# When finished activation tiles are written out to DRAM: four chunks after their first product in place of 28

## The chip, the cores and the metric

The kernel runs on one core of a Trainium2 chip. The metric is the time on the device in microseconds (us), the median of several runs. A run's time is a little longer than its span, the stretch that the profiler records.

## The reference, cut to what matters

One layer of a streaming encoder on 512 tokens of width 1024. A mixer (convolutions and a gated recurrence) comes first; behind it stands a retrieval over 128 × 128 = 16384 small "experts". Each token needs 8 × 16 of them:

```python
idx = ...                      # (tokens, 8 heads, 16): experts chosen by a two-stage top-16
g = softmax(best_s)            # their gates
u_sel = expert_u[idx]
act = gelu(einsum('phkd,pd->phk', u_sel, xb))
coef = g * act
return einsum('phk,phkd->pd', coef, expert_v[idx])
```

`expert_u` and `expert_v` are tables of 16384 × 1024 numbers, 64 MB each.

## The kernel before, in words

The 512 tokens are split. For 192 of them the chosen rows of the tables are gathered one by one (indirect DMAs issued by POOL, tile `rows`) and multiplied on DVE (`scr` at L918 for the u table, `ys` at L935 for the v table). For the other 320 the kernel computes densely: it takes the u table in 128 chunks of 128 experts, forms all products of a chunk with the 320 tokens on TensorE (PE), applies the gelu, multiplies by a gate that is zero for experts that were not chosen, and multiplies by the chunk of the v table.

The work follows a list `jobs`: chunks 0 to 123 of u come first ("u phase"); then the 128 chunks of v ("v phase"), with the last four chunks of u between the first of them. Around job k the program is written out by hand, and each engine keeps that order:

- `w_ahead` lets the SP queue issue the 512 KB loads of table chunks, five or six jobs ahead, into a ring of four buffers `wraw` (L70; in the v phase every fifth goes to a buffer `raw`, L962, and chunks 5 to 11 of u go straight into `whi` or `wlo` buffers, L957).
- `w_high(k + 3)` lets ACT round the chunk to its high half `whi` (L75); `w_low(k + 2)` lets DVE form the low half `wlo` (L80). Both rings have four buffers, so a half of chunk k can be written once PE is done with chunk k − 4, and a `wraw` buffer is free once DVE has made the low half.
- `u_chunk(k)` issues 24 matmuls into `ps_act` (L89 to L91, or L1011 in chunks 1 to 11), and then `u_evict` puts the gelu of the chunk before into SBUF (ACT, L1002). Two chunks share one tile `act`, a pair: 128 × 640 numbers, 320 KB. There are 16 such tiles.
- The v phase begins with pair 48. Pairs 0 to 47 are written to DRAM (`spill`, L992, tensor `Ad`, issued by SP) and read again later in the v phase (`v_act`, L1064). Pairs 48 to 63 stay in SBUF.

Beside this, DVE and ACT search the top-16 lists and build the gate tables, which go out to DRAM through SP (`Gd<-stg`, L786). At the end of the u phase SP fetches the first gates (`gt<-Gd`, L1051, six loads of 512 KB) and later ones in loads of 1 MB (`h<-Gd`, L1038). In the v phase `v_gated` forms the coefficients `cf` (ACT L1072, DVE L1074), `v_high` and `v_rest` split them into `ch` (ACT, L1081) and `cl` (DVE, L1088), and PE adds up `acc` (L1197), 18 matmuls for a chunk. In both phases DVE's program has steps of the gathers (`scr`, `ys`) between the others.

SP is one queue: it issues its DMAs in program order, and one that has to wait holds up those behind it. All DMAs share the 16 DMA engines.

In `u_chunk(c)` for an even chunk c, `spill(q)` is called with q = c // 2 − RB // 2 + 2; RB is 32, so pair q goes out in chunk 2q + 28. The condition `0 <= q < v0 // 2` with v0 = 96 limits it to pairs 0 to 47.

Of the kernel before, what the change touches and what calls it, by code (L numbers as in the profile page):

```python
# [34 lines left out]
def block_kernel(ctx, tc, xT, small, w_ada1, w_ada, b_ada, w_in, w_r, w_i, w_out, w_q, keys, uT, u, v, final_g, out):  # L35
# [51 lines left out]
    def mm3(ps, hi, lo, xh, xl, ks, first, last):  # L87
        for k in ks:
            nc.tensor.matmul(ps, hi[:, k, :], xh(k), start=first and k == ks[0], stop=False)  # L89
            nc.tensor.matmul(ps, hi[:, k, :], xl(k), start=False, stop=False)  # L90
            nc.tensor.matmul(ps, lo[:, k, :], xh(k), start=False, stop=last and k == ks[-1])  # L91
# [300 lines left out]
    for cb in range(4):  # L392
# [26 lines left out]
        q = mt("q")  # L419
# [571 lines left out]
    def spill(q):  # L991
        nc.sync.dma_start(Ad[q], act[q].rearrange("p c t -> p (c t)"))  # L992
        act[q] = None
# [3 lines left out]
    def u_evict():  # L997
        if unread:
            c, ps = unread.pop()
            if c % 2 == 0:  # L1000
                act[c // 2] = ring.tile([128, 2, NU], F32, name="act", bufs=RB // 2)
            nc.scalar.activation(act[c // 2][:, c % 2], ps, AF.Gelu)  # L1002

    def u_chunk(k, pool):
        c = jobs[k][1]
        if c:
            ps = pool.tile([128, NU], F32, name="ps_act", bufs=3 if pool is psE else 2)
            if k < FN:
                raw = wraw.pop(k)
                for j in range(KB):  # L1010
                    nc.tensor.matmul(ps, raw[:, j, :], h2f[j // 2][:, j % 2], start=j == 0, stop=j == KB - 1)  # L1011
            else:
                mm3(ps, whi.pop(k), wlo.pop(k), hd, ld, range(KB), True, True)
            u_evict()
            unread.append((c, ps))
        q = c // 2 - RB // 2 + 2
        if c % 2 == 0 and 0 <= q < v0 // 2:
            spill(q)
        pe[0] += FPE if c and k < FN else 3530
        dve[0] += 0 if c and k < FN - 2 else 1140  # L1020
        ac[0] += 450 if c and k < FN - 3 else 1400
# [104 lines left out]
    for k in range(CE):  # L1126
        weights(k)
        u_chunk(k, psE)
        if k >= CE - 2:
            (v_gated, v_high)[k - CE + 2](0)  # L1130
# [83 lines left out]
    for k in range(CE, len(jobs)):  # L1214
        kind, n = jobs[k]
        w_ahead(k)
        if kind == "v" and n % 2 == 0:
            v_high(n // 2 + 1)
        w_high(k + 3)
        w_low(k + 2)  # L1220
        if kind == "u":
            u_chunk(k, psP)
        else:
            q, e = divmod(n, 2)
            v_gates(n + 5)
            if e == 0:
                v_act(q + 4)
            else:
                v_rest(q + 1)
                v_gated(q + 2)  # L1230
            vsp[n] = [w.pop(k).rearrange("p k e -> p (k e)") for w in (whi, wlo)] + [c[:, e] for c in coef[q]]
            if n < NE - VT:
                for b in range(3):
                    v_chunk(n, b)
                del vsp[n]
            u_evict()
            pe[0] += 4090
            dve[0] += 2005
        if kind == "v":
            paced = n + 1 + UV * min(n + 1, NE - CE)  # L1240
            share = min(paced / (NE - VE + UV * (NE - CE)), 1) * (steps + 0.31 * (NE - RB)) - 0.31 * max(n + 1 - RB, 0)
            while done < share and next(sparse, None):
                done += 1
# [64 lines left out]
RB = 32  # L1308
# [54 lines left out]
```

## Time and profile before

| | |
|---|---|
| median of 3 runs | 1352.85 us (1352.3 to 1353.4) |
| the profiled execution's own time | 1352.07 us |
| its span | 1350.3 us |
| PE busy | 1305.1 us, 97% of the span |
| DVE busy | 1226.2 us, 91% |
| ACT, POOL busy | 727.3 us, 496.7 us |
| moved by DMA | 440.57 MB, mean 326 GB/s |
| spills: 48 DMAs of 320 KB | issued from 400.2 to 795.1 us |
| first and last gelu of the u chunks in the profile | 289.4 us, 825.4 us |

Engines run beside each other, so the busy shares do not add up to one. A matmul's end is modelled in the profile, and a busy PE is not always a PE at its full rate; PE's idle time says where it waited.

### The profile page before, as it was taken

How to read it: one execution, taken by the hardware profiler on the slowest of the kernel's cores; microseconds unless marked ns; L12 is line 12 of the kernel's file. 1: busy time of each engine (PE TensorE's matmuls, PEld its weight loads, DVE VectorE, ACT ScalarE, POOL GpSimd, SP SyncE). 2: the span in 40 equal slices, each digit the busy share in tenths (PEclk: the TensorE clock that was granted, in tenths of full speed). 3: DMA queues.
4: the chain of work that ended last, by engine and by line, in shares of the span. 5: the costliest groups of instructions: out<-in, count | busy, mean ns of one | idle time of the engine just before them, and what ended most of it. 6: DMA issues, size and time to landing. Idle time of an engine off the chain costs nothing.

```text
span 1350.3 us, 21168 instructions
## 1 busy us (share of the span) xinstructions
PE 1305.1 (97%) x7408; PEld 1119.9 (83%) x7408; DVE 1226.2 (91%) x2272; ACT 727.3 (54%) x1318; POOL 496.7 (37%) x336
## 2 busy tenths in 40 slices
PE   5999999999899999999999999899999999999996
PEld 2678776777899999999999988788888888888884
DVE  6899875989999999999998669899989989999998
ACT  4677735424686987878668543333443333333333
POOL 0000000000243123456655527577656555644540
PEclk9999999999999999999999999899999999999998
DMA  9684542251798899999999999999999999999993
GB/s 360 237 296 150 175 134 84 72 205 32 264 330 311 320 332 364 395 402 404 418 408 418 417 349 399 365 393 416 413 415 413 416 412 413 411 408 413 387 358 141
DMA packets 149375, 440.57 MB, mean 326 GB/s; under 512 B 14994, under 2 KB 42642, under 8 KB 149268
## 3 DMA queue, kind: packets, MB, share of 16 engines
q1 hardware_dynamic: 102116, 267.75, 53.0%
q0 software_dynamic: 46864, 170.41, 32.2%
q8 instruction: 58, 0.95, 0.3%
q10 hardware_dynamic: 288, 1.05, 0.2%
q14 instruction: 49, 0.40, 0.1%
HBM read 394.07 MB, written 45.09 MB: 325 GB/s over the span
## 4 chain that ended last, share of the span: by engine, by line
PE 59%; DVE 21%; issue 9%; DMA 7%; POOL 2%; ACT 2%; DVEq 0%; POOLq 0%; ACTq 0%; SPq 0%
PE acc L1197 34%; DVE wlo L80 5%; PE ps_z L89 5%; PE ps_z L90 4%; PE ps_z L91 4%; DVE scr L918 3%; DMA rows<-in_u_dram,idx_s 3%; PE ps_act L89 2%; PE ps_act L90 2%; DVE oh L729 2%; PE ps_act L91 2%; POOL rows L897 2%; DMA wraw<-in_v_dram 1%; DVE rep L544 1%; DMA wraw<-in_uT_dram 1%
## 5 line engine op out<-in xcount | busy, mean ns | idle before, releaser
L75 ACT ACTIVATE whi<-wraw 128x1024 fp32r<-128x1024 f32 x255 | 269.8, 1059 | 252.9 <-PE acc L1197 98.3
L80 DVE TENSOR_TENSOR wlo<-wraw,whi 128x1024 fp32r<-128x1024 f32 x255 | 310.7, 1219 | 57.4 <-ACT whi L75 56.7
L89 PE MATMUL ps_act<-h,whi 128*128 128x320 f32 x928 | 291.9, 315 | 0.0
L91 PE MATMUL ps_act<-h,wlo 128*128 128x320 f32 x928 | 287.3, 310 | 0.9 <-DVE wlo L80 0.9
L90 PE MATMUL ps_act<-h,whi 128*128 128x320 f32 x928 | 287.2, 310 | 0.0
L897 POOL DMA_INDIRECT rows<-in_u_dram,idx_s x128 | 206.0, 1610 | 153.6 <-DVE scr L918 124.4
L897 POOL DMA_INDIRECT rows<-in_v_dram,idx_s x128 | 192.3, 1502 | 163.1 <-DVE ys L935 144.3
L1197 PE MATMUL acc<-whi,cl 128*128 128x512 f32 x750 | 232.4, 391 | 4.3 <-DVE cl L1088 4.3
L1197 PE MATMUL acc<-whi,ch 128*128 128x512 f32 x750 | 232.5, 391 | 2.5 <-ACT ch L1081 2.5
L1197 PE MATMUL acc<-wlo,ch 128*128 128x512 f32 x750 | 231.9, 390 | 0.0
L89 PEld LDWEIGHTS ps_act<-h,whi 128*128 128x128 f32 x928 | 174.7, 188 | 1.3
L91 PEld LDWEIGHTS ps_act<-h,wlo 128*128 128x128 f32 x928 | 174.6, 188 | 1.2 <-DVE wlo L80 1.1
L90 PEld LDWEIGHTS ps_act<-h,whi 128*128 128x128 f32 x928 | 174.8, 188 | 0.2
L897 POOL DMA_INDIRECT rows<-in_u_dram,idx_b x64 | 92.1, 1439 | 219.4 <-DVE scr L918 156.7
L1197 PEld LDWEIGHTS acc<-whi,cl 128*128 128x128 f32 x750 | 141.5, 189 | 34.2 <-DVE cl L1088 4.7
L1197 PEld LDWEIGHTS acc<-whi,ch 128*128 128x128 f32 x750 | 141.5, 189 | 32.1 <-ACT ch L1081 2.8
L1197 PEld LDWEIGHTS acc<-wlo,ch 128*128 128x128 f32 x750 | 141.6, 189 | 29.6
L935 DVE SCALAR_TENSOR_TENSOR ys<-rows,acts,ys 128x1024 f32<-128x1024 f32 x127 | 163.3, 1286 | 1.4
L918 DVE SCALAR_TENSOR_TENSOR scr<-rows,h2n 128x1024 f16<-128x1024 f32 x128 | 156.3, 1221 | 5.4 <-DMA rows<-in_u_dram,idx_s 3.8
L1081 ACT ACTIVATE ch<-cf 128x768 fp32r<-128x768 f32 x64 | 54.2, 847 | 103.7 <-issue 67.1
L1002 ACT ACTIVATE act<-ps_act 128x320 f32<-128x320 f32 x127 | 56.0, 441 | 87.0 <-PE ps_act L91 52.4
L750 ACT ACTIVATE igh<-oh,gl 128x128 f16<-128x128 f16 x320 | 99.5, 433 | 3.8 <-DVE oh L729 3.8
(308 smaller groups left out, 1859.9 us busy)
## 6 DMA issues: line engine op xcount, KB each, us to landing
wraw<-in_uT_dram SPq DMA_DIRECT2D x120, 512.0 KB, 8.0
wraw<-in_v_dram SPq DMA_DIRECT2D x103, 512.0 KB, 12.3
Gd<-stg SPq DMA_DIRECT2D x46, 512.0 KB, 10.2
wada<-in_w_ada_dram SPq DMA_DIRECT2D x45, 512.0 KB, 5.4
Ad<-act SPq DMA_DIRECT2D x48, 320.0 KB, 11.2
act<-Ad SPq DMA_DIRECT2D x48, 320.0 KB, 13.6
raw<-in_v_dram SPq DMA_DIRECT2D x25, 512.0 KB, 13.5
h<-Gd SPq DMA_DIRECT2D x12, 1024.0 KB, 18.8
```

The lines of the kernel that those rows point to most:

```text
L75: nc.scalar.activation(hi, raw, AF.Copy)
L80: nc.vector.tensor_sub(lo, raw, hi.bitcast(F32))
L89: nc.tensor.matmul(ps, hi[:, k, :], xh(k), start=first and k == ks[0], stop=False)
L90: nc.tensor.matmul(ps, hi[:, k, :], xl(k), start=False, stop=False)
L91: nc.tensor.matmul(ps, lo[:, k, :], xh(k), start=False, stop=last and k == ks[-1])
L750: nc.scalar.activation(ig[:, 1, k // 2, :, k % 2], of[:, k // 2, 0, :, k % 2], AF.Copy, scale=gl[:, t0 + k:t0 + k + 1])
L897: nc.gpsimd.indirect_dma_start(out=r[:, :], out_offset=None, in_=table, in_offset=bass.IndirectOffsetOnAxis(ap=idxs[:, k:k + 1], axis=0))
L918: nc.vector.scalar_tensor_tensor(scr, rows.pop(n), 1.0, hn, op0=OP.mult, op1=OP.mult, accum_out=dst[:, k:k + 1])
L935: nc.vector.scalar_tensor_tensor(ys, rows.pop(k), acts[:, k:k + 1], ys, op0=OP.mult, op1=OP.add)
L1002: nc.scalar.activation(act[c // 2][:, c % 2], ps, AF.Gelu)
L1081: nc.scalar.activation(ch, coef[q], AF.Copy)
L1197: nc.tensor.matmul(accs[b][e], st[:, bs], mv[:, e * 512:(e + 1) * 512], start=first, stop=last)
```

## The change

The index of the pair that is spilled in an even chunk c becomes c // 2 − 2. Pair q goes out in chunk 2q + 4 in place of 2q + 28.

```diff
-        q = c // 2 - RB // 2 + 2
+        q = c // 2 - 2
         if c % 2 == 0 and 0 <= q < v0 // 2:
             spill(q)
```

Its tile is complete when the second gelu of the pair is done, which the program issues in chunk 2q + 2. The 48 spills stay the same in size and number. They stood in chunks 28 to 122 and now stand in chunks 4 to 98. The orders of PE, DVE, ACT and POOL are the same before and after, row for row; SP's is the only one that changes.

SP's order at the start of the u phase, before. `whi<-in_uT` and `wlo<-in_uT` are loads of chunks 5 to 11, `wraw<-in_uT` are loads of later chunks, `Gd<-stg` is a store of gates, and `Ad<-act` is a spill:

```order
L957 DMA whi<-in_uT_dram 128x1024
L70 DMA wraw<-in_uT_dram 128x1024 x15
L786 DMA Gd_2622<-stg 128x1024 x2
L70 DMA wraw<-in_uT_dram 128x1024 x4
L786 DMA Gd_2622<-stg 128x1024 x2
L70 DMA wraw<-in_uT_dram 128x1024 x3
L992 DMA Ad<-act 128x640
```

The same place after, from the load of chunk 9 on:

```order
L957 DMA whi<-in_uT_dram 128x1024
L992 DMA Ad<-act 128x640
L957 DMA wlo<-in_uT_dram 128x1024
L957 DMA whi<-in_uT_dram 128x1024
L992 DMA Ad<-act 128x640
L70 DMA wraw<-in_uT_dram 128x1024 x2
L992 DMA Ad<-act 128x640
L70 DMA wraw<-in_uT_dram 128x1024 x2
```

After each second load there is now a spill from chunk 4 on, where before 22 loads of `wraw` and two pairs of gate stores came first; twelve spills now stand in chunks 4 to 26, where there was none.

SP's order at the end of the u phase, before. `wraw<-in_v` is a load of a v chunk, `gt<-Gd` fetches the first gates, one load for each of three blocks of 128 tokens:

```order
L992 DMA Ad<-act 128x640
L70 DMA wraw<-in_uT_dram 128x1024 x2
L992 DMA Ad<-act 128x640
L70 DMA wraw<-in_v_dram 128x1024
L1051 DMA gt<-Gd_2623 128x8x128
L1051 DMA gt<-Gd_2624 128x8x128
L1051 DMA gt<-Gd_2622 128x8x128
L70 DMA wraw<-in_uT_dram 128x1024
L70 DMA wraw<-in_v_dram 128x1024
L992 DMA Ad<-act 128x640
```

The same place after:

```order
L70 DMA wraw<-in_uT_dram 128x1024 x3
L786 DMA Gd_2622<-stg 128x1024 x2
L70 DMA wraw<-in_uT_dram 128x1024 x7
L70 DMA wraw<-in_v_dram 128x1024
L1051 DMA gt<-Gd_2623 128x8x128
L1051 DMA gt<-Gd_2624 128x8x128
L1051 DMA gt<-Gd_2622 128x8x128
L70 DMA wraw<-in_uT_dram 128x1024
L70 DMA wraw<-in_v_dram 128x1024
```

The twelve spills of chunks 100 to 122 are gone from between the loads there; the loads and the gate fetches keep their order. Between chunks 28 and 98 every even chunk has one spill as before, only of a younger pair.

## The prediction

> **What bounds the kernel now.** I read the page first, then the stages in windows, then PE's waits by stage, and last SP, ACT and DVE around those waits.
>
> ```profile
> span 1350.3 us, 21168 instructions
> PE 1305.1 (97%) x7408; PEld 1119.9 (83%) x7408; DVE 1226.2 (91%) x2272; ACT 727.3 (54%) x1318; POOL 496.7 (37%) x336
> Ad<-act SPq DMA_DIRECT2D x48, 320.0 KB, 11.2
> ```
>
> PE is idle for 45.2 us of 1350.3, so no change of DMA order can bring more than that. The next rows are windows (us from the start: length, busy time of PE, PEld, DVE, ACT and POOL, then PE's granted clock, DMA share and GB/s).
>
> ```profile
> 284.00:340.00 56.00, 56.00 (x245) 41.78 (x243) 54.32 (x321) 18.18 (x27) 3.54 (x5) 1.00 0.27 87
> 340.00:400.00 60.00, 56.13 (x436) 55.11 (x435) 59.83 (x167) 43.01 (x107) 19.21 (x15) 0.97 0.87 297
> 400.00:690.00 290.00, 288.52 (x2246) 282.58 (x2245) 280.34 (x513) 225.50 (x493) 122.08 (x79) 1.00 0.97 370
> 690.00:796.00 106.00, 102.74 (x753) 99.01 (x753) 80.12 (x103) 74.07 (x188) 46.32 (x30) 0.98 1.02 398
> 796.00:870.00 74.00, 69.71 (x332) 59.50 (x331) 64.81 (x90) 25.98 (x36) 45.16 (x30) 0.95 1.00 389
> 870.00:1318.00 448.00, 448.00 (x1978) 370.95 (x1977) 423.79 (x432) 171.87 (x222) 255.25 (x166) 1.00 1.02 404
> ```
>
> The DMA engines are nearly empty until 340 us (share 0.27), and full from 690 us (1.02). PE loses 3.9 us at 340 to 400, 3.3 at 690 to 796 and 4.3 at 796 to 870, and nothing after that until 1318. The three large losses, from PE's waits in the windows 330 to 360, 770 to 800 and 850 to 870 (in all, times, longest):
>
> ```profile
> PE ps_gt L762 <- DVE igh L743: 3.0, 1, 3.0
> PE acc L1197 <- ACT ch L1081: 2.5, 1, 2.5
> PE acc L1197 <- DVE cl L1088: 4.3, 1, 4.3
> ```
>
> **The change, part by part.** Only SP's order changes. From chunk 28 to 98 each even chunk has a spill in both versions, so the middle costs nothing: the DMA work there is the same. What moves is 12 spills out of the end and 12 into the start. Issues with their size and median us to landing, first two rows from 690 to 796 us, then 400 to 690, then 284 to 400; the last row is ACT's wait for u weights from 680 to 800:
>
> ```profile
> Ad<-act SPq DMA_DIRECT2D x12, 320.0 KB, 14.5
> wraw<-in_uT_dram SPq DMA_DIRECT2D x21, 512.0 KB, 12.6
> Ad<-act SPq DMA_DIRECT2D x36, 320.0 KB, 9.9
> wraw<-in_uT_dram SPq DMA_DIRECT2D x22, 512.0 KB, 6.0
> ACT whi L75 <- DMA wraw<-in_uT_dram: 23.7, 11, 4.5
> ```
>
> A spill moves 327,680 bytes; at the 398 GB/s of the full window that is 0.82 us of all engines, and 12 are 9.9 us. So in the 106 us from 690 to 796 a tenth of the DMA work goes. There a weight load takes 12.6 us to land, against 6.0 early, and ACT waits for it eleven times, 23.7 us.
>
> *The first stall at the end of the u phase.* ACT's rows (start, length, and in brackets the idle time before and what ended it):
>
> ```profile
> 770.31 1.06 ACT L75 ACTIVATE whi<-wraw 128x1024 fp32r<-128x1024 f32 x1 [3.15 <-DMA wraw<-in_uT_dram]
> 787.06 0.31 ACT L1072 ACTIVATE cf<-gt 128x128 f32<-128x128 f32 x1 [3.00 <-DMA gt<-Gd]
> 790.27 1.06 ACT L75 ACTIVATE whi<-wraw 128x1024 fp32r<-128x1024 f32 x1 [2.91 <-DMA wraw<-in_uT_dram]
> 791.55 0.83 ACT L1081 ACTIVATE ch<-cf 128x768 fp32r<-128x768 f32 x1
> ```
>
> `ch` is what PE waited for, and ACT came to it late because it had waited for DMA each time before: for weights, for the gates, for weights again. SP's rows show where those loads came from:
>
> ```profile
> 772.66 0.33 SPq L70 DMA_DIRECT2D wraw<-in_v_dram  x1
> 773.34 9.27 SPq L1051 DMA_DIRECT2D gt<-Gd  x3
> 782.71 1.34 SPq L70 DMA_DIRECT2D wraw<-in_uT_dram  x1
> 795.12 0.43 SPq L992 DMA_DIRECT2D Ad<-act  x1
> ```
>
> The gate fetch could be issued only behind the load at 772.66, which needed a `wraw` buffer, which was free only when the late halves had been formed. The load at 782.71 is the one ACT waits for at 790.27. With 9.9 us less DMA work over these 28 chunks the halves are no longer late, and the fetch moves forward with them. `ch` has to come 2.55 us earlier for the stall to go; single waits of about 3 us stand in its way, so I take it that it goes. Its price is more than the wait. PE's rows, then PE's window rows with the granted clock:
>
> ```profile
> 792.44 1.22 PE L1197 MATMUL acc<-whi,ch 128*128 128x512 f32 x2 [2.55 <-ACT ch L1081]
> 795.17 0.69 PE L1197 MATMUL acc<-whi,ch 128*128 128x512 f32 x2
> 862.39 1.22 PE L1197 MATMUL acc<-whi,cl 128*128 128x512 f32 x2 [4.29 <-DVE cl L1088]
> 866.82 0.70 PE L1197 MATMUL acc<-wlo,ch 128*128 128x512 f32 x2
> 790.00:795.00 5.00, 2.56 (x6) 2.08 (x7) 3.60 (x4) 4.18 (x7) 0.00 (x0) 0.69 1.08 362
> 860.00:865.00 5.00, 2.61 (x6) 2.13 (x7) 4.69 (x6) 3.27 (x5) 0.39 (x1) 0.51 1.02 415
> ```
>
> After each wait PE ran with a lower granted clock (0.69 and 0.51 in these windows). From 792.44 to 795.17 it did three pairs in 2.73 us; at full clock a pair takes 2 × 448 / 1978 = 0.453 us (the window 870 to 1318), so 1.37 us were lost on top. The first stall costs 2.55 + 1.37 = 3.92 us. The second: five pairs in 4.43 us from 862.39 to 866.82 against 2.27, so 4.29 + 2.16 = 6.45 us. Gain of the first stall: 3.92; bounds 0 (the fetch moves with nothing) and 3.92.
>
> [...]
>
> *The second stall.* DVE's rows, and the last from the chain of waits (start, us, what):
>
> ```profile
> 795.37 1.22 DVE L918 SCALAR_TENSOR_TENSOR scr<-rows,h2n 128x1024 f16<-128x1024 f32 x1
> 806.32 1.23 DVE L918 SCALAR_TENSOR_TENSOR scr<-rows,h2n 128x1024 f16<-128x1024 f32 x1 [0.77 <-DMA rows<-in_u_dram,idx_s]
> 808.78 1.23 DVE L918 SCALAR_TENSOR_TENSOR scr<-rows,h2n 128x1024 f16<-128x1024 f32 x1 [1.22 <-DMA rows<-in_u_dram,idx_s]
> 839.54 19.25 DMA wraw<-in_v_dram
> ```
>
> DVE begins its gather steps at 795.37 and works almost without a gap until 839; then the chain is a v load of 19.25 us, whose low half stands in DVE's order ahead of the `cl` that PE needs. All of this moves earlier with PE's start of the v phase, so in itself the stall stays as long. What helps is that the spill issued at 795.12 no longer stands among the gathers DVE waits for (0.77 + 1.22 us): its 0.82 us. I take 0.8. The bounds are 6.45, all of it, and −3.92: DMA from 796 on is full (1.00), so what PE gains at the first stall can be waited for here.
>
> *The start.* Twelve spills now share the DMA engines with the loads of chunks 10 to 31. A spill waits for the second gelu of its pair and holds up the loads behind it in SP; but those loads are several chunks ahead of PE and wait themselves for buffers that come free only later, and up to 340 us the engines are 73% empty. The tender place is the stall at 351 to 354 (rows of ACT, DVE and PE):
>
> ```profile
> 351.26 1.06 ACT L75 ACTIVATE whi<-wraw 128x1024 fp32r<-128x1024 f32 x1 [0.98 <-DMA wraw<-in_uT_dram]
> 353.89 0.68 DVE L743 TENSOR_TENSOR igh<-oh,gh 128x1024 f16<-128x1024 f16 x1
> 354.63 1.60 PE L762 MATMUL ps_gt<-igh,oh 128*128 128x128 f16 x16 [3.01 <-DVE igh L743]
> ```
>
> DVE is busy 59.83 of 60 us here and brings `igh` late by its own work. But ACT also waits 0.98 us for weights just before, so a spill ahead of that load can cost its 0.82 us. No gain is possible, since nothing leaves this stretch; at most two spills lie close ahead, 1.64 us. DVE being the nearer limit, I take a loss of 0.4.
>
> *Tails.* The release of an `act` tile comes 24 chunks earlier and saves nothing: no gelu waited for a spill. The reads back from `Ad` begin far behind the last write in both.
>
> Sum: 3.92 + 0.8 − 0.4 = 4.3 us, so the profiled execution's 1352.07 us would become 1347.8. The median of the runs lies 0.78 above that execution: 1348.5 us.
>
> **The rivals.**
>
> *Both stalls go.* For it: DVE's idle time at 690 to 796 (26 of 106 us) is mostly waiting for late halves. Against it: in the last chunks of the u phase its order holds little but those halves, so it cannot run far ahead. 1352.85 − 3.92 − 6.45 + 0.4 = 1342.9 us.
>
> *The gain is paid back at the second stall, or the first stays.* For it: DMA is full from 796 to 870 and SP spends 9.27 us on three gate fetches whoever else is there. Against it: the bytes between the two stalls do not grow. With 3.92 won and 3.92 lost, and 0.4 at the start: 1353.2 us; about no change.
>
> *Slower.* The early spills push the weights of chunks 17 to 20 back while ACT, DVE and PE hang on each other at 340 to 356, and the end wins nothing. Four spills stand in chunks 12 to 18; if each adds its 0.82 us to that chain, it is 3.3 us and 1356.1 us. It decides when a load there lands over 2.7 us later than before. Against it: DVE's own work ends that wait. [...]
>
> That the change does nothing is no rival: SP's order shows it done.
>
> **How the numbers follow.** About 0.2%, 2.7 us, is what a measurement of this kernel can tell from no change, so faster means under 1350.2. My forecast, the first stall gone and the second about as it was, has 0.45 (its own range 1346.3 to 1350.4); both gone 0.13; paid back or not moved 0.25; slower at the start 0.17. Faster: 0.42 of the first and 0.13, together 0.55. Slower: most of the last and a little of the third, 0.18. The rest is 0.27. The range holds the first three cases: 1342.5 to 1354.0.
>
> **What would show it.** Right: no idle time of PE before its first `acc`, clock 1.00 there; ACT's waits for u weights from 680 to 800 well below 23.7 us; spills ending near 690 us; twelve spills before 400 us; PE's wait at 354 within 1 us of 3.0. Wrong: the `acc` wait for `ch` still there although ACT's weight waits are gone (then the gate fetch sets it), or the second wait grown towards 8 us, or a new wait of PE between 300 and 400 us.

## The result, and the profile after

The changed kernel takes 1343.22 us (median of 7 runs, 1339.6 to 1347.4) against 1352.85 (7 runs, 1350.2 to 1353.8). The ratio is 0.9932, with an interval of 0.9917 to 0.9947: 9.2 us or 0.7%, twice the 4.3 us that were forecast. The medians differ by 9.6 us, and beside the experiments below the kernel before took 1350.8 to 1351.2 us, so the gain is known to about 1 us. The profiled execution took 1342.4 us. Its page:

```profile
span 1340.6 us, 21127 instructions
PE 1299.7 (97%) x7408; PEld 1116.4 (83%) x7408; DVE 1226.3 (91%) x2272; ACT 727.3 (54%) x1318; POOL 498.8 (37%) x336
Ad<-act SPq DMA_DIRECT2D x48, 320.0 KB
```

PE's busy time fell by 5.4 us with the same number of matmuls. Part of this is the slow clock behind the two waits (1.37 + 2.16 us in the prediction's count), but not all: the first hint that part of the gain had stood inside "busy" and not in idle time. The windows (columns as in the prediction):

```profile
284.00:340.00 56.00, 55.76 (x237) 41.30 (x233) 54.81 (x321) 18.18 (x26) 3.96 (x5) 1.00 0.36 116
340.00:400.00 60.00, 56.35 (x437) 55.58 (x438) 59.83 (x168) 43.27 (x107) 18.82 (x14) 0.97 0.94 334
400.00:690.00 290.00, 287.44 (x2238) 281.45 (x2237) 279.70 (x511) 224.67 (x490) 121.25 (x78) 1.00 0.98 370
690.00:796.00 106.00, 106.00 (x795) 104.18 (x794) 87.92 (x114) 76.73 (x190) 51.25 (x35) 1.00 1.02 392
796.00:870.00 74.00, 72.16 (x344) 61.07 (x343) 66.73 (x92) 26.71 (x38) 45.15 (x31) 1.00 0.99 382
870.00:1308.00 438.00, 437.39 (x1928) 361.08 (x1927) 413.93 (x420) 168.41 (x217) 253.22 (x162) 1.00 1.03 406
```

From 690 to 796 us PE is never idle now, and 795 matmuls are recorded in place of 753 (a few can be missing from a trace). The DMA engines are as full as before (1.02). PE's waits in the windows 330 to 360 and 800 to 870 (from 690 to 800 there is none), and ACT's wait for u weights from 680 to 800, which was 23.7 us before:

```profile
PE ps_gt L762 <- DVE igh L743: 3.0, 1, 3.0
PE acc L1197 <- DVE cl L1088: 1.8, 1, 1.8
ACT whi L75 <- DMA wraw<-in_uT_dram: 1.5, 1, 1.5
```

**Where the 9.7 us between the two spans came from.** Six starts cut the span into pieces: the gelus of u chunks 1, 53 and 97, the first `acc`, the last gelu of a u chunk and the last `acc` of L1197 (other lines add up the last chunk; this start is read to 0.1 us).

| piece | before | after | difference |
|---|---|---|---|
| start to gelu 1 | 289.43 | 288.94 | −0.49 |
| gelu 1 to 53 (twelve spills come in) | 216.99 | 217.13 | +0.14 |
| gelu 53 to 97 | 179.92 | 181.00 | +1.08 |
| **gelu 97 to first `acc`** (twelve spills leave) | 106.10 | 100.26 | **−5.84** |
| **first `acc` to last gelu** (slow clock, then none) | 32.95 | 31.50 | **−1.45** |
| **last gelu to last `acc`** (holds the second wait) | 499.21 | 496.07 | **−3.14** |
| last `acc` to the end | 25.70 | 25.70 | 0.00 |

The piece from 53 to 97 varies from 178 to 182 us among all the executions below, whatever the spills do there. The −5.84 holds more than the 2.55 us wait. In before, two steps of the gate matmuls `ps_gt` are slow (PE's rows, with the next `ps_act` matmul behind each):

```profile
722.80 0.23 PE L762 MATMUL ps_gt<-igh,oh 128*128 128x128 f16 x1
723.53 2.24 PE L762 MATMUL ps_gt<-igh,oh 128*128 128x128 f16 x15 [0.50 <-ACT igh L750]
725.58 0.39 PE L89 MATMUL ps_act<-h,whi 128*128 128x320 f32 x1
...
745.24 2.35 PE L762 MATMUL ps_gt<-igh,oh 128*128 128x128 f16 x16
747.40 0.39 PE L89 MATMUL ps_act<-h,whi 128*128 128x320 f32 x1
```

The same step after, and PE's next row:

```profile
744.10 1.10 PE L762 MATMUL ps_gt<-igh,oh 128*128 128x128 f16 x16
745.00 0.39 PE L89 MATMUL ps_act<-h,whi 128*128 128x320 f32 x1
```

From its start to the next matmul the step takes 0.90 us after, but 2.78 and 2.16 us before. The excess, 1.88 and 1.26 us, is shown as idle for 0.50 us only. The reason stands in ACT's rows; for the second step, before first:

```profile
743.89 1.06 ACT L75 ACTIVATE whi<-wraw 128x1024 fp32r<-128x1024 f32 x1 [1.99 <-DMA wraw<-in_uT_dram]
744.86 2.47 ACT L750 ACTIVATE igh<-oh,selB 128x128 f16<-128x128 f16 x8
```

```profile
741.06 2.48 ACT L750 ACTIVATE igh<-oh,selB 128x128 f16<-128x128 f16 x8
```

ACT forms eight `igh` tiles in 2.5 us. In before it came to them late, having waited 1.99 us for weights, and PE took each pair of matmuls as its tile appeared (744.86 to 747.33 beside 745.24 to 747.40): it was starved but looked busy. In after the tiles are ready at 743.54, before PE's step. The first step is alike: ACT begins its tiles at 723.00 us in before and at 720.48 in after. So 2.55 + 1.88 + 1.26 = 5.69 of the 5.84 us are accounted for.

### The profile page after: what moved, and what is told of

Read it like the earlier page. It is cut to its first block, busy times and chain, and to the rows that moved or that the text cites. A ratio compares the mean times of both kernels' runs of the same rounds, so it can differ in the third digit from the quotient of the medians.

```text
span 1340.6 us, 21127 instructions
## 1 busy us (share of the span) xinstructions
PE 1299.7 (97%) x7408; PEld 1116.4 (83%) x7408; DVE 1226.3 (91%) x2272; ACT 727.3 (54%) x1318; POOL 498.8 (37%) x336
## 4 chain that ended last, share of the span: by engine, by line
PE 63%; DVE 21%; issue 7%; DMA 6%; ACT 2%; POOL 0%; DVEq 0%; SPq 0%; ACTq 0%; POOLq 0%
PE acc L1197 26%; PE ps_act L89 6%; PE ps_act L91 6%; PE ps_act L90 6%; DVE wlo L80 5%; PE ps_z L89 5%; PE ps_z L90 5%; DVE scr L918 5%; PE ps_z L91 4%; DMA wraw<-in_v_dram 3%; DMA wraw<-in_uT_dram 2%; PE ps_gt L762 2%; DVE oh L729 2%; DVE cl L1088 1%; DVE rep L544 1%
## 5 line engine op out<-in xcount | busy, mean ns | idle before, releaser
L897 POOL DMA_INDIRECT rows<-in_v_dram,idx_s x128 | 196.9, 1538 | 157.8 <-DVE ys L935 139.0
L1197 PE MATMUL acc<-whi,cl 128*128 128x512 f32 x750 | 231.5, 390 | 2.4 <-DVE cl L1088 2.4
L1197 PE MATMUL acc<-wlo,ch 128*128 128x512 f32 x750 | 231.0, 389 | 0.0
L1197 PE MATMUL acc<-whi,ch 128*128 128x512 f32 x750 | 231.0, 389 | 0.0
L1197 PEld LDWEIGHTS acc<-whi,cl 128*128 128x128 f32 x750 | 140.2, 188 | 33.3 <-DVE cl L1088 4.5
L1197 PEld LDWEIGHTS acc<-wlo,ch 128*128 128x128 f32 x750 | 140.8, 188 | 29.4
L1197 PEld LDWEIGHTS acc<-whi,ch 128*128 128x128 f32 x750 | 140.6, 188 | 28.9
```

The source lines that it names most:

```text
L897: nc.gpsimd.indirect_dma_start(out=r[:, :], out_offset=None, in_=table, in_offset=bass.IndirectOffsetOnAxis(ap=idxs[:, k:k + 1], axis=0))
L1197: nc.tensor.matmul(accs[b][e], st[:, bs], mv[:, e * 512:(e + 1) * 512], start=first, stop=last)
```

## The experiments

The first question was whether the bytes at the end do it, the number of DMAs there, or something at the start. A "dummy write" below is a copy of an `act` tile to a scratch tensor `Xd`, at the place in SP's order where a spill stood. Each ratio is against runs of the kernel before that were made beside it (medians 1350.8 to 1351.2 us).

**end_full.** The changed kernel with twelve dummy writes of 320 KB where before had its last twelve spills:

```diff
+    Xd = dram.tile([12, 128, 2 * NU], F32, name="Xd")
...
+        if c % 2 == 0 and 100 <= c <= 122:
+            nc.sync.dma_start(Xd[c // 2 - 50], act[c // 2 - 2].rearrange("p c t -> p (c t)"))
```

> The changed kernel, and in chunks 100 to 122 twelve extra writes of 320 KB of a live pair to an unread DRAM tensor, where the twelve late spills had stood. Theory (the DMA work of the full stretch 690 to 796 us is what counts): everything comes back; ACT waits over 18 us for u weights from 680 to 800, PE waits about 2.5 us before its first acc, the second wait is about 4 us, gate matmuls stall; 1350 to 1355 us. Rival A (the gain comes from writing the pairs early, whatever else runs late): stays at 1343 us, give or take 3.

Measured: 1351.31 us, ratio 1.000 (0.9989 to 1.0012). The gain is wholly gone. PE's waits from 740 to 800 us, and ACT's for u weights:

```profile
PE ps_gt L762 <- ACT igh L750: 0.8, 1, 0.8
PE acc L1201 <- ACT ch L1085: 1.9, 1, 1.9
ACT whi L75 <- DMA wraw<-in_uT_dram: 23.3, 11, 3.5
```

Both losses are back, and ACT waits for weights as in before (23.7 us). The piece up to the first `acc` takes 105.89 us. One expectation failed: the second wait, expected at about 4 us, is 1.31 us here.

**end_tiny.** The same, with 8 KB each:

```diff
-            nc.sync.dma_start(Xd[c // 2 - 50], act[c // 2 - 2].rearrange("p c t -> p (c t)"))
+            nc.sync.dma_start(Xd[c // 2 - 50][:, 0:16], act[c // 2 - 2][:, 0, 0:16])
```

> The same twelve extra writes at the same places, but of 8 KB each in place of 320. Theory (bytes): as the changed kernel, 1343 us give or take 3; ACT's waits for u weights from 680 to 800 below 5 us. Rival B (what counts is the number of DMAs that stand in SP's queue and take part in its turns, not their bytes): at least half of the gain is gone, 1348 us or more.

Measured: 1342.94 us, ratio 0.994 (0.992 to 0.9961), and 100.24 us up to the first `acc`. The same twelve DMAs, with the same waits for the gelu and the same places in SP's queue, cost nothing. Nor is it the number of packets, which is 151103 in both traces; in end_tiny 1536 more of them are under 512 B. It is the bytes; whether as many bytes read would do the same was not tried. ACT's row, a little over the 5 us that were expected at most:

```profile
ACT whi L75 <- DMA wraw<-in_uT_dram: 5.3, 7, 1.1
```

**start_only.** The kernel before, with twelve dummy writes in chunks 4 to 26, where the change puts its first twelve spills; the end stays as before:

```diff
+        if c % 2 == 0 and 4 <= c <= 26:
+            nc.sync.dma_start(Xd[c // 2 - 2], act[c // 2 - 2].rearrange("p c t -> p (c t)"))
```

> The kernel before, and twelve extra writes of 320 KB in chunks 4 to 26, where the change puts its twelve early spills. Theory: the start has room, so the time is that of before, 1352.9 us (nothing to 0.5 us more); the wait of PE at 354 us stays at 3.0. The prediction's term for the start: 0.4 us more, at most 1.6. Rival (the early spills cost up to 3.3 us, which a larger gain at the end hides): 1355 to 1356 us.

Measured: 1351.79 us, ratio 1.0001 (0.9988 to 1.0014). From 340 to 400 us PE is busy as long as in before, and its wait for `igh` is the same:

```profile
340.00:400.00 60.00, 56.13 (x436) 55.08 (x436) 59.83 (x174) 42.07 (x102) 19.42 (x16) 0.97 0.93 334
PE ps_gt L762 <- DVE igh L743: 3.0, 1, 3.0
```

The start costs nothing that can be seen; the interval, about 2 us to either side, would hide a few tenths. The profiled execution of this kernel was its slowest run (1357.86 us), with a second wait of 4.7 us.

**end_dropped.** The kernel before, without the twelve late spills and with nothing in their place:

```diff
-            spill(q)
+            if q < 36:
+                spill(q)
+            else:
+                act[q] = None
...
-                nc.sync.dma_start(act[c].rearrange("p c t -> p (c t)"), Ad[c])
+                nc.sync.dma_start(act[c].rearrange("p c t -> p (c t)"), Ad[c if c < 36 else c - 12])
```

> The kernel before without the twelve spills of chunks 100 to 122; the reads of those pairs in the v phase take the place of a pair twelve lower, so the numbers of these 24 chunks are wrong and the amount of reading is the same. Nothing is added at the start. Theory: as the changed kernel, 1343 us give or take 3, with the first acc not waiting. Rival A (writing early): 1352 us.

Measured: 1341.3 us, ratio 0.9923 (0.9898 to 0.9948), and 100.26 us up to the first `acc`. Taking the bytes out of the end is enough for the whole gain, with the start untouched.

**near_gone and far_gone.** Is it only the spills close to the gate fetch, or the backlog of the whole stretch? near_gone keeps spills at chunks 100 to 110 and has none at 112 to 122; far_gone is the reverse:

```diff
-        q = c // 2 - 2
+        q = c // 2 - 8
```

```diff
-        q = c // 2 - 2
-        if c % 2 == 0 and 0 <= q < v0 // 2:
+        q = c // 2 - (8 if c < 100 else 50 if c < 112 else 14)
+        if c % 2 == 0 and 0 <= q < v0 // 2 and not 100 <= c < 112:
```

> The changed kernel with q = c // 2 - 8: the 48 spills stand in chunks 16 to 110, so the six of chunks 112 to 122, beside the gate fetches, are gone and the six of chunks 100 to 110 stand as before. Theory (DMA time of the whole full stretch, shared out over two kinds of PE loss): the gate matmuls of chunks 104 to 111 still stall as before, about 3 us, but PE does not wait before its first acc; from the gelu of chunk 97 to the first acc about 103 us (before 106.1, after 100.3); 1346 to 1349 us. Rival (only what stands beside the gate fetch counts): the whole gain, 1343 us and 100.3 us.

> The other six: the spills of chunks 100 to 110 are gone, those of chunks 112 to 122 stand as before (the six pairs moved instead go out from chunk 16 on). Theory: the gate matmuls do not stall, but ACT is late again at the first gates and PE waits 1 to 2.5 us before its first acc; about 102 to 103.5 us from the gelu of chunk 97 to the first acc; 1346 to 1350 us. Rival (only what stands beside the gate fetch counts): nothing gained, 1351 us and 106 us.

Measured: near_gone 1348.44 us, ratio 0.9976 (0.9958 to 0.9994); far_gone 1346.23 us, 0.9969 (0.9954 to 0.9984). Each takes a part, inside the expected times, so the rival that only the spills beside the gate fetch count falls. The pieces up to the first `acc` missed their expectations (about 103 us, and 102 to 103.5), and so did far_gone's `ch` wait (1 to 2.5). Waits of PE in near_gone, then in far_gone, from 690 us to the first `acc`:

```profile
PE ps_gt L762 <- ACT igh L750: 1.3, 1, 1.3
```

```profile
PE acc L1197 <- ACT ch L1081: 0.8, 1, 0.8
```

They divide the loss. The early six make the gate matmuls late and keep the piece at 104.83 us though no `ch` wait is left. Without them the gate matmuls run clean and 0.76 us of the `ch` wait stays, 101.18 us. In this piece the early six are worth 4.9 of the 5.8 us and the late six 1.3: here the backlog delayed whatever came next behind it, and the `ch` wait was only its last place. A part of near_gone's loss is clock: two steps of its gate matmuls take 1.45 and 3.61 us in place of 0.90, and behind the second PE ran at half clock from 749.66 to 753.07 us, which makes 0.67 on average in the window there (columns as before):

```profile
748.00:753.00 5.00, 4.86 (x26) 4.04 (x26) 2.06 (x3) 5.00 (x17) 0.94 (x1) 0.67 1.03 420
```

The steps' excess of 3.26 us and about 1.5 us for the clock, an estimate from half of the 2.95 us behind the step, come to 4.7, close to the 4.6 us that the piece is over after's.

**end_double.** The kernel before, with a dummy write beside each of its twelve late spills:

```diff
+        if c % 2 == 0 and 100 <= c <= 122:
+            nc.sync.dma_start(Xd[c // 2 - 50], act[c // 2 - 2].rearrange("p c t -> p (c t)"))
```

> The kernel before, with a second write of 320 KB (a live pair, to an unread tensor) behind each of the twelve spills of chunks 100 to 122. Theory (the stretch is bound by DMA): twelve more writes are 9.9 us of DMA time and PE has no lead left to hide it; the stretch from the gelu of chunk 97 to the first acc grows from 106 to 113 to 116 us; 1358 to 1363 us. Rival (the late spills only upset an order once, more of them costs little): under 1354 us.

Measured: 1361.56 us, ratio 1.0087 (1.0064 to 1.0109), 114.11 us up to the first `acc`. Its `ch` wait has doubled:

```profile
PE acc L1201 <- ACT ch L1085: 5.1, 1, 5.1
```

So 9.9 us of DMA time more (12 × 327,680 bytes at 398 GB/s, the prediction's estimate) lengthened the piece by 8.0 us, and 9.9 us less shortened it by 5.84. In this piece there is nothing left to win in after: six kernels share the value 100.24 to 100.26 us.

**The second wait: uv0, last_two, fetch_pool.** In after 1.84 us of it are left. PE's row, DVE's first gather step after the u phase, and a piece of the chain of waits:

```profile
853.38 0.73 PE L1197 MATMUL acc<-whi,cl 128*128 128x512 f32 x2 [1.84 <-DVE cl L1088]
```

```profile
788.08 1.22 DVE L918 SCALAR_TENSOR_TENSOR scr<-rows,h2n 128x1024 f16<-128x1024 f32 x1
```

```profile
831.27 18.78 DMA wraw<-in_v_dram
```

DVE starts its run of gather steps 7.29 us earlier (795.37 before), PE its first `acc` 5.11 us earlier, and behind them stands a v load of 19 us as before. Three edits of the changed kernel try to move this wait. uv0 changes a constant that shares out DVE's gather steps among the chunks; last_two puts dummy writes back at chunks 120 and 122 alone, among the gathers DVE waits for; fetch_pool lets POOL issue the three 1 MB gate fetches that hold SP ahead of that v load:

```diff
-UV = 0.86
+UV = 0.0
```

```diff
+        if c in (120, 122):
+            nc.sync.dma_start(Xd[c // 2 - 60], act[c // 2 - 2].rearrange("p c t -> p (c t)"))
```

```diff
-                nc.sync.dma_start(g16[m][:, 8 * t - 8:8 * t], Gd[t][:, :, cc:cc + 16, :].rearrange("g j i t -> j g i t"))
+                (nc.gpsimd if m == 16 else nc.sync).dma_start(g16[m][:, 8 * t - 8:8 * t], Gd[t][:, :, cc:cc + 16, :].rearrange("g j i t -> j g i t"))
```

> The changed kernel with UV = 0 in place of 0.86: about eight gather steps fewer stand in the first eight jobs of the v phase, spread over the later ones. For the second wait. Theory C (it comes from DMA being full there, half of it gathers): the wait for cl goes, and the time from the gelu of chunk 127 to the last acc is at most 494 us in its profile (before 499.2, after 496.1); 1340 to 1342 us. Rival D (SP held by the 1 MB gate fetches keeps the v load from being issued): no change, 1343 us, or slower because DVE has more to do later.

> The changed kernel and two extra writes of 320 KB of a live pair in chunks 120 and 122, the places of the two last spills before. For the second wait. Theory E (the prediction's term: late spills stand among the gathers that DVE waits for at the start of the v phase): from the gelu of chunk 97 to the first acc stays within 1 us of 100.3; DVE waits for rows again, 1 to 2 us, and the second wait is 2 us or more, with the clock down behind it; from the gelu of chunk 127 to the last acc 497 us or more; 1345 to 1348 us. Rival F (the second wait grows out of the late halves of the whole stretch before): as the changed kernel, 1343 us give or take 3, second wait at most 2 us.

> The changed kernel with the three 1 MB fetches of the gates of v chunks 16 to 31 issued by POOL in place of SP, so that SP is not held by them and the v load of 18.8 us can be issued up to 5 us earlier. Theory D (SP's hold makes the second wait): the wait for cl is gone, from the gelu of chunk 127 to the last acc at most 494 us, 1340 to 1342 us. Theory C (the DMA engines are full there, whoever issues): no change, 1343 us give or take 3; slower, up to 1347, if POOL's own gathers are held.

Measured: uv0 1341.46 us, ratio 0.993 (0.9908 to 0.9953); last_two 1343.53, 0.9934 (0.9913 to 0.9956); fetch_pool 1344.47, 0.9954 (0.9931 to 0.9977). After's own ratio, 0.9932, lies in all three intervals, so the times tell none of them from after. Behind the last gelu uv0 comes near the 494 us that its theory C expected (494.51), fetch_pool not to the 494 of theory D (497.11). The window from 796 to 870 in uv0, then in last_two:

```profile
796.00:870.00 74.00, 74.00 (x354) 63.04 (x354) 64.81 (x89) 28.77 (x40) 42.80 (x27) 1.00 0.96 363
```

```profile
796.00:870.00 74.00, 74.00 (x356) 63.27 (x356) 69.06 (x94) 27.81 (x38) 47.48 (x32) 1.00 1.02 397
```

PE loses nothing there in either, though last_two has the two spills back (495.03 us behind the last gelu, where theory E expected 497 or more): that they were what DVE waited for is not borne out. Later, at 978.54 us, PE does wait 1.60 us for `cl` in last_two, and 0.83 us at 976.80 in uv0. In fetch_pool there is a wait of 2.8 us, but it ends at 837.47 and none ends near 853, and DVE waits for rows (770 to 845 us), which it does not in after:

```profile
PE acc L1197 <- DVE cl L1088: 2.8, 1, 2.8
DVE scr L918 <- DMA rows<-in_u_dram,idx_s: 7.6, 3, 4.1
```

Two rows of POOL, the first fetch and the second:

```profile
817.73 0.95 POOL L1038 DMA_DIRECT2D h<-Gd  x1 [4.11 <-PE ps_act L91]
820.91 0.95 POOL L1038 DMA_DIRECT2D h<-Gd  x1
```

POOL stood still for 4.11 us ahead of the first, and the gather that follows the second is the one DVE waits for until 834.17. The edit took a hold away from SP and put one on POOL, so it does not settle whether SP's hold set the wait of after. The runs side by side (us; the second column is ACT's waiting for u weights from 680 to 800, the `cl` column all of PE's waits for `cl` added up):

| kernel | ACT waits | gelu 97 to first `acc` | `ch` wait | `cl` waits | last gelu to last `acc` | ratio |
|---|---|---|---|---|---|---|
| before | 23.7 | 106.10 | 2.55 | 4.29 | 499.21 | 1 |
| after | 1.5 | 100.26 | 0 | 2.46 | 496.07 | 0.9932 |
| end_full | 23.3 | 105.89 | 1.95 | 3.00 | 496.67 | 1.000 |
| end_tiny | 5.3 | 100.24 | 0 | 0 | 493.60 | 0.994 |
| start_only | 22.9 | 105.41 | 1.46 | 6.45 | 503.26 | 1.0001 |
| end_dropped | 0 | 100.26 | 0 | 0.67 | 494.06 | 0.9923 |
| near_gone | 9.0 | 104.83 | 0 | 1.21 | 494.62 | 0.9976 |
| far_gone | 14.8 | 101.18 | 0.76 | 2.18 | 496.52 | 0.9969 |
| end_double | 22.3 | 114.11 | 5.12 | 2.70 | 496.83 | 1.0087 |
| uv0 | 6.8 | 100.26 | 0 | 1.21 | 494.51 | 0.993 |
| last_two | 0.9 | 100.26 | 0 | 1.60 | 495.03 | 0.9934 |
| fetch_pool | 1.3 | 100.26 | 0 | 2.79 | 497.11 | 0.9954 |

The piece up to the first `acc` follows the bytes, and repeats to 0.02 us where few or none are there. The `cl` waits do not: with the same twelve writes they are 3.00 in end_full and 6.45 in start_only (the second wait itself 1.31 and 4.67). One execution of each kernel does not say what its mean is.

## Why the prediction was right or wrong

- **The mechanism: right for the first stall.** Removing 9.9 us of DMA work from a full stretch is what counts (end_full against end_tiny, end_dropped). Every sign named for the first stall came: no idle time before the first `acc`, the clock at 1.00, ACT's weight waits down from 23.7 to 1.5 us. The last spill went out at 682.3 us.
- **The DMA engines did not empty, though.** Totals from 690 to 796 us, and the gathers and u loads issued there, in before and then in after:

```profile
DMA packets 17224, 42.16 MB, mean 398 GB/s; under 512 B 1351, under 2 KB 7142, under 8 KB 17214
wraw<-in_uT_dram SPq DMA_DIRECT2D x21, 512.0 KB, 12.6
rows<-in_u_dram,idx_s POOLq DMA_INDIRECT x30, 9.3
```

```profile
DMA packets 16776, 41.60 MB, mean 392 GB/s; under 512 B 1265, under 2 KB 7409, under 8 KB 16766
wraw<-in_uT_dram SPq DMA_DIRECT2D x22, 512.0 KB
rows<-in_u_dram,idx_s POOLq DMA_INDIRECT x35
```

  Of the 3.9 MB of spills 3.4 were replaced by later work that came forward; the issues show five more gathers, one more u load and three more v loads (six in place of three).
- **The first stall: right that it goes, mis-sized.** Its term, "2.55 + 1.37 = 3.92 us", was the wait that the profile names and the slow clock behind it. The two pieces around it measured 5.84 + 1.45 = 7.29 us. What was missing is the 3.1 us of gate matmuls that waited, all but 0.50 us of it inside "busy". The prediction took PE's time as lost only where the profile showed it idle (3.26 us from 690 to 796) or at a lower clock just behind, while this window has 42 matmuls fewer on record than the same 106 us after. The upper bound of that term, 3.92, was therefore no bound, and neither was "PE is idle for 45.2 us, so no change of DMA order can bring more".
- **The second stall: "0.8 us" was too low, its cause not settled.** Its reasoning, the spill at 795.12 among the gathers, is not borne out by last_two. It also took the wait as shifted unchanged; after shows 1.84 us without slow clock, and in these traces the length of a wait did not tell whether the clock falls (last section). Of the 3.14 us between the two traces 1.83 are `cl` waits (4.29 to 2.46) and about 2.2 the slow clock of before; about 0.9 went the other way and is not placed. The piece behind the last gelu has a mean of 499.0 us in the four executions with all twelve late writes and 495.1 in the six with none or two, and the two sets overlap (496.67 against 497.11). From the ratio, 9.2 − 7.3 leaves about 2 us, an estimate that is no surer than the 9.2.
- **The start: no sign of the "loss of 0.4".** ACT's wait for weights grew, PE's 3.0 us wait is the same to 0.01 us, and the piece from gelu 1 to 53 grew by 0.14 us. That DVE's own work hid ACT's wait fits DVE's 59.83 busy us of 60, and was not tested by itself. ACT's row in after (0.98 us before):

```profile
351.45 1.06 ACT L75 ACTIVATE whi<-wraw 128x1024 fp32r<-128x1024 f32 x1 [1.64 <-DMA wraw<-in_uT_dram]
```

  The rivals "paid back" and "slower at the start" fall with start_only and end_tiny.
- **The number.** 1348.5 was 5.3 us too high. The measured 1343.22 lies outside the forecast's own 1346.3 to 1350.4 and only 0.7 us inside the lower end of the whole range, which the rival with both stalls gone had stretched that far: that the range held is luck more than insight. That rival gave 1342.9, near the 1343.22 measured, but for another reason: it put 6.45 us on the second wait and nothing on the gate matmuls.
- **The gate fetch moved forward** as the prediction said. SP's row now (773.34 and 9.27 us before), and ACT's two that led to the stall:

```profile
769.19 6.29 SPq L1051 DMA_DIRECT2D gt<-Gd  x3
```

```profile
782.59 1.06 ACT L75 ACTIVATE whi<-wraw 128x1024 fp32r<-128x1024 f32 x1 [1.46 <-DMA wraw<-in_uT_dram]
784.34 0.84 ACT L1081 ACTIVATE ch<-cf 128x768 fp32r<-128x768 f32 x1
```

  `ch` stands ready at 785.18 us, and PE comes to its first `acc` at 787.33: 2.15 us of room.

## What to carry to other kernels

Move writes that nobody is waiting for out of a stretch in which the DMA engines are full (share 1.02 here): 9.9 us of such writes cost 7.3 us of PE's time at the end of the u phase here, and nothing that could be measured from 284 to 400 us, where the DMA share rose from 0.27 to 0.34 and from 0.87 to 0.93 with them (start_only). The price of a backlog is not the last wait that the profile names: compare how long the same matmul step takes from its start to the next matmul in a quiet and in a crowded place, since PE, fed tile by tile, stood in before's profile as busy for 2.35 us with a step that takes 1.10 us in after's. Where a wait scatters from kernel to kernel as the second one does here (0 to 4.7 us), no single execution prices it; use several runs of kernels that differ in one thing.

## What the runs showed of the hardware

In these traces the length of a wait alone does not say whether PE's granted clock falls behind it. Behind a wait of 1.95 us in end_full, ended at 794.17, it was 0.71, and behind one of 1.84 us in after, ended at 853.38, it was 1.00 (PE and the others, with the clock in the column after POOL):

```profile
793.00:798.00 5.00, 3.83 (x11) 2.85 (x12) 4.88 (x5) 4.38 (x8) 0.00 (x0) 0.71 1.03 314
853.00:858.00 5.00, 4.62 (x20) 3.83 (x21) 4.93 (x8) 3.17 (x4) 2.10 (x2) 1.00 0.73 297
```

Between 340 and 400 us PE stands idle for 3.7 to 3.9 us in all twelve kernels; in before, after, start_only and uv0 the wait for `igh` makes 3.0 us of it. The granted clock of that window is 0.97 in seven of them and 1.00 in five (end_full, end_double, uv0, last_two, fetch_pool). In uv0:

```profile
357.59 1.08 PE L762 MATMUL ps_gt<-igh,oh 128*128 128x128 f16 x16 [3.00 <-DVE igh L743]
356.00:361.00 5.00, 3.41 (x33) 3.40 (x33) 5.00 (x7) 5.00 (x16) 0.91 (x1) 1.00 0.75 256
```

In before the clock stood at half in exactly these stretches between 284 and 1318 us:

```profile
354.97:358.38 3.41, 3.41 (x22) 3.41 (x20) 3.41 (x5) 3.41 (x11) 1.15 (x1) 0.50 0.50 153
791.87:795.29 3.42, 2.85 (x7) 2.27 (x8) 3.39 (x4) 2.87 (x6) 0.00 (x0) 0.50 1.10 338
860.14:866.97 6.83, 4.58 (x11) 3.62 (x12) 6.66 (x9) 3.22 (x5) 2.06 (x2) 0.50 0.81 329
```

The waits with their clock, from the rows and windows of each trace:

| run | wait of PE in us, ended at | granted clock there |
|---|---|---|
| before | 3.01, 354.63 | 0.50 from 354.97 to 358.38 |
| before | 2.55, 792.44 | 0.50 from 791.87 to 795.29 |
| before | 4.29, 862.39 | 0.50 from 860.14 to 866.97 |
| after | 3.02, 354.17 | 0.50 from 355 to 357 |
| end_full | 1.95, 794.17 | 0.71 from 793 to 798 |
| far_gone | 2.18, 855.77 | 0.69 from 855 to 860 |
| after | 1.84, 853.38 | 1.00 from 853 to 858 |
| end_full | 1.31, 861.46 | 1.00 from 861 to 866 |
| start_only | 1.46, 795.58 | 1.00 from 795 to 800 |
| uv0 | 3.00, 357.59 | 1.00 from 356 to 361 |

In near_gone the clock was down (0.67 from 748 to 753 us) where PE had waited 1.3 us for `igh` and the gate matmuls were fed tile by tile. So in these traces the clock was down at waits of 1.3 to 4.3 us and held at others of 1.3 to 3.0 us; what decides it is not shown, since no run here shifts a wait on purpose. Whether a wait of 2 or 3 us costs clock on top can't be told from its length here, which is one more reason not to price it from one execution.
